# Direct tiles ahead of the products, value products in one step, full column transposes, and weight sums through GpSimd's queue: one edit to a one-layer encoder kernel

## The chip, the core and the metric

The kernel runs on one NeuronCore of a Trainium2 chip. The time is the device time of one execution in microseconds (us). Three runs of the kernel as it was gave 2321.19, 2312.80 and 2321.06 us, a median of 2321.06 us. A fourth execution was recorded by the hardware profiler, and every row of a profile below is from such a recording.

The engines are named as the profile names them: PE (TensorE's matmuls), PEld (its weight loads), DVE (VectorE), ACT (ScalarE), POOL (GpSimd) and SP (the queue of SyncE, from which most DMA transfers start). Each engine runs its instructions in its own fixed order. An instruction that has to wait holds back everything behind it on the same engine.

## What is computed

One layer of a streaming encoder is applied to a prompt of 2048 rows and to 8 short samples of 16 rows (one more tile of 128 rows), 1024 features wide:

```
z = x @ w_in                        # q, k, v, output gate, 8 gate columns, attention q, k, v
hm = mlstm_chunkwise(...)           # 4 heads x 128, carries a matrix state from chunk to chunk
ha = sliding-window attention(...)  # 8 query heads, 2 key/value heads x 64, with sinks
h = layer_norm(alpha * x + concat(hm, ha) @ w_out)
y = layer_norm(alpha * h + conv_ffn(h))   # up 1024 -> 5632, causal conv, silu gate, down 2816 -> 1024
```

All of it is float32. Large products are made from three matmuls on split operands (a high part and a remainder of each operand), so every operand of PE is first split: ACT writes the high part and DVE the remainder. The groups of large products are also made with seven block products instead of eight, in the manner of Strassen and Winograd, so sums of blocks of x and of the weights have to be made beforehand. These sums are DVE's work.

## The kernel before

**Stages.** The input products (stage I, function `i_dense`) go over 4 blocks of 512 rows (block 0 has the sample tile as well). Each block goes through 5 groups of weight columns (g = 0 to 4), and a group is seven block products with the numbers 1 to 7 (s). Beside them stand the "direct" tiles (`i_direct`, 24 matmuls of 264 columns, L730): the gate columns, the attention keys and the attention values of 128 rows. Then come the output product with the first layer norm (`o_block`), the up projection (matmuls at L1873) and the down projection (L2083).

**Chains.** While the input and output products run, two chains of small steps are woven between them: `m_chain` for the mLSTM and `a_chain` for the attention, each tile after tile (16 prompt tiles). A chain is a generator. At each `yield` it says what its step costs PE, how long its next step should wait, and how many of the 5 rotating PSUM banks it needs. `Chains.weave` keeps a planned time and takes a step when both wait and banks are due (`HOLDS` is the planned time that a bank stays in use). So the order of PE's instructions is fixed by this plan when the program is built. If an operand is late on the chip, PE stands still.

**The start.** Before the change `i_begin` puts tiles 2 and 3 of block 0 first (L343), then product (0,0,1), the sample tile, and the other products. Tiles 0 and 1 of a block come at the end of that block, together with tiles 2 and 3 of the next (L362 to L364). `i_dense` writes out the loads of the start by hand (L592 to L615): weights of the direct tiles (`next_raw`, `next_split`), the four raw quarters of x (`x_load`, buffers `xr1` to `xr4`, 512 KB each), and their splits and sums (`x_steps`). The `passages` (L618) say after which product of the last group each split or sum for the next block is made.

**Attention.** In `swa` (L1271) the scores of a tile are softmaxed; then the weights are transposed for each of the two key tiles (`ppt`, L1342), copied by ACT (`pth`, L1343), and multiplied with the values (`ppo`, L1348). The product for one key tile comes one step after its transposes, so the value products of a tile are two groups of 4 PE instructions with other work between. They use half of the array's columns (64 of 128). `scores` also copies a sink column into the score buffer on GpSimd (L1297).

**mLSTM columns.** `m_cols` (L1020) transposes a row buffer `ay` of 36 partitions into columns (`pcol`, L1024), once for each of 17 tiles. `m_rows` sends a row vector to DRAM and back, spread over all partitions, through GpSimd's queue (`zM` at L1078, `wi` at L1080), and the next tile's `m_masked` (L1109, DVE) reads `wi`.

**Weight sums.** `d_sums` (L840) prepares sums of the down projection's weights for the third stage: step 0 loads two pieces of 512 KB (`txy`), step 1 makes four subtractions on DVE (L850 to L853), step 2 stores both (`zt`). There are 11 of these: 4 in each of blocks 2 and 3, at products 6, 5 and 3 (6, 2 and 5 in group 3), and 3 in the output stage. All of them use the raw buffers `xr1` and `xr3` and SP's queue, so the load of one waits for the store of the one before it.

Of the kernel before, what the change touches and what calls it, by code (L numbers as in the profile page):

```python
# [34 lines left out]
HOLDS = {"pm": 6500, "pgr": 4000, "pnum": 5000, "ppo": 6500}  # L35
# [169 lines left out]
class Prog:  # L205
# [131 lines left out]
    def i_begin(self):  # L337
# [196 lines left out]
    def x_load(self, b, *qs):  # L534
        for q in qs:
            self.xr[b, q] = r = self.x_raw(q)
            self.nc.sync.dma_start(r, self.a["xq"][b][(q - 1) // 2, (q - 1) % 2])

    def x_steps(self, b, *steps):
# [3 lines left out]
        for s in steps:  # L543
# [14 lines left out]
            else:  # L558
# [3 lines left out]
                n = 4 if (b, s) == (0, "b12") else 1  # L562
# [24 lines left out]
    def i_dense(self):  # L587
# [5 lines left out]
        self.x_load(0, 2)  # L593
        for _ in range(3):
            self.next_raw()
        self.x_load(0, 4)
# [3 lines left out]
        self.rope_load(IBLOCKS[0][2], 2)  # L600
# [12 lines left out]
        self.x_steps(0, 2, "t3", 7, "t2", 6)  # L613
# [4 lines left out]
        passages = [{1: ["load"], 7: ["t3", 7], 6: ["t2", 6], 3: [3, "t4"], 4: ["b12", "t1"]},  # L618
                    {1: ["load"], 6: ["t3"], 7: [7, "t2"], 5: [6], 3: [3, "t4"], 4: ["b12", "t1"]}]
        sums = 0  # L620
        after = None
        for item in self.items:
# [9 lines left out]
            if item[0] == "t":  # L632
# [33 lines left out]
            if (g, s) == (1, 6):  # L666
                self.rope_load(IBLOCKS[b][0], 2)
            if g == last and b + 1 < nb:
                if s == 7:
                    self.rope_load(IBLOCKS[b + 1][2], 2)  # L670
# [11 lines left out]
            if b >= nb // 2 and g < last:  # L682
# [1503 lines left out]
```

## Time and profile before

| | us |
|---|---|
| runs | 2321.19, 2312.80, 2321.06 |
| median | 2321.06 |
| profiled execution, its own time | 2316.15 |
| its span, first to last instruction | 2314.3 |
| mean granted clock of PE | 0.996 |
| moved by DMA in the span | 632.38 MB, mean 273 GB/s |

In this execution the direct tiles ran at 5.9 to 17.2 us (tiles 2 and 3), 21.3 to 24.4 (the sample tile), 155 to 167, 290 to 302 and 455 to 467 (four tiles each) and 623 to 629 us (the last two). The output stage began at 628.8 us on PE.

How to read the rows. In a timeline a row is: start in us, duration in us, engine, line, operation, output <- inputs, shape, count of instructions merged into the row, and in brackets the idle time of the engine just before and what ended it. A matmul's duration includes its way through the array, so that matmuls overlap; what one costs is seen from the start of the next. In a table of windows each engine has its busy time in the stretch, then come the granted clock of PE (1.00 is full speed), the share of the time in which the DMA engines were busy, and GB/s. In a row of a tile or a line the three numbers are shortest, median and longest in ns.

### The profile page before, as it was taken

How to read it: one execution, taken by the hardware profiler on the slowest of the kernel's cores; microseconds unless marked ns; L12 is line 12 of the kernel's file. 1: busy time of each engine (PE TensorE's matmuls, PEld its weight loads, DVE VectorE, ACT ScalarE, POOL GpSimd, SP SyncE). 2: the span in 40 equal slices, each digit the busy share in tenths (PEclk: the TensorE clock that was granted, in tenths of full speed). 3: DMA queues.
4: the chain of work that ended last, by engine and by line, in shares of the span. 5: the costliest groups of instructions: out<-in, count | busy, mean ns of one | idle time of the engine just before them, and what ended most of it. 6: DMA issues, size and time to landing. Idle time of an engine off the chain costs nothing.

```text
span 2314.3 us, 39788 instructions
## 1 busy us (share of the span) xinstructions
PE 2281.9 (99%) x14293; PEld 2094.9 (91%) x14293; DVE 1808.1 (78%) x3075; ACT 1269.0 (55%) x2377; POOL 279.5 (12%) x509
## 2 busy tenths in 40 slices
PE   8999999999999999999999999999999999999998
PEld 8999989989877778999999999999999978888876
DVE  8777687787688888998788777678766786895987
ACT  5453466776766655555656555555555544444442
POOL 0001000000011212121002000013111200100200
PEclk9999999999999999999999999999999999999999
DMA  7888999999977757888778889978898776756743
GB/s 276 287 308 297 301 309 336 314 310 342 315 269 240 240 201 270 303 319 311 276 289 274 306 304 311 315 264 287 312 294 261 225 282 208 261 175 215 255 157 108
DMA packets 300166, 632.38 MB, mean 273 GB/s; under 512 B 47869, under 2 KB 141121, under 8 KB 299969
## 3 DMA queue, kind: packets, MB, share of 16 engines
q1 hardware_dynamic: 295296, 616.14, 77.9%
q0 software_dynamic: 3520, 10.56, 1.4%
q10 hardware_dynamic: 1152, 3.15, 0.4%
q8 instruction: 113, 1.85, 0.3%
q14 instruction: 85, 0.69, 0.1%
HBM read 458.11 MB, written 171.64 MB: 272 GB/s over the span
## 4 chain that ended last, share of the span: by engine, by line
PE 76%; DVE 5%; DMA 4%; issue 2%; ACT 1%; SPq 0%; POOL 0%; DVEq 0%; ACTq 0%; POOLq 0%
PE dps L1873 19%; PE fup L1873 19%; PE dps L704 7%; PE dps L2083 6%; PE fht L2083 6%; PE fup L2083 6%; PE dps L222 2%; PE dps L224 2%; PE dps L223 2%; PE ppo L1348 1%; PE psc L1303 1%; PE ppt L1342 1%; DVE w L218 1%; PE fht L1697 1%; DMA txy<-wdn 0%
## 5 line engine op out<-in xcount | busy, mean ns | idle before, releaser
L1873 PE MATMUL dps<-hh,uw 128*128 128x384 f32 (+1 forms) x1848 | 478.7, 328 | 2.0 <-DVE u L1904 2.0
L1873 PE MATMUL fup<-hh,uw 128*128 128x384 f32 (+1 forms) x1848 | 478.2, 328 | 1.5 <-ACT ua L1894 1.5
L1873 PEld LDWEIGHTS dps<-hh,uw 128*128 128x128 f32 x1848 | 330.5, 188 | 2.2 <-DVE u L1904 2.2
L1873 PEld LDWEIGHTS fup<-hh,uw 128*128 128x128 f32 x1848 | 330.0, 188 | 2.0 <-ACT ua L1894 1.9
L1930 DVE SCALAR_TENSOR_TENSOR cc<-u,cw,cc 128x768 f32<-128x768 f32 (+1 forms) x264 | 258.1, 978 | 64.9 <-ACT cc L1928 55.5
L1873 PE MATMUL fup<-hl,uw 128*128 128x384 f32 (+1 forms) x924 | 302.5, 327 | 1.7 <-DVE hl L218 1.7
L1873 PE MATMUL dps<-hl,uw 128*128 128x384 f32 (+1 forms) x924 | 302.8, 328 | 0.0
L704 PE MATMUL dps<-w,oh 128*128 128x256 f32 x1344 | 254.3, 284 | 0.7 <-DVE zev L777 0.7
L217 ACT CAST uw<-wraw 128x1024 fp32r<-128x1024 f32 x126 | 123.0, 979 | 223.8 <-PE dps L2083 120.1
L218 DVE TENSOR_TENSOR w<-wraw,w 128x1024 fp32r<-128x1024 f32 (+2 forms) x167 | 189.4, 1141 | 56.1 <-ACT w L217 48.9
L217 ACT CAST w<-wraw 128x1024 fp32r<-128x1024 f32 (+2 forms) x167 | 163.0, 985 | 107.3 <-PE dps L704 38.9
L704 PEld LDWEIGHTS dps<-w,oh 128*128 128x128 f32 x1344 | 210.5, 188 | 11.8 <-issue 8.1
L218 DVE TENSOR_TENSOR uw<-wraw,uw 128x1024 fp32r<-128x1024 f32 x126 | 142.4, 1131 | 65.7 <-ACT uw L217 65.5
L704 PE MATMUL dps<-w,ol 128*128 128x256 f32 x672 | 187.8, 279 | 0.0
L704 PE MATMUL dps<-oh,w 128*128 128x256 f32 x896 | 170.9, 285 | 6.6 <-ACT mr L1153 3.8
L1873 PEld LDWEIGHTS fup<-hl,uw 128*128 128x128 f32 x924 | 173.5, 188 | 2.4 <-DVE hl L218 2.3
L2083 PE MATMUL fup<-uw,fu 128*128 128x512 f32 x726 | 174.2, 396 | 0.6 <-DVE uw L218 0.6
L1873 PEld LDWEIGHTS dps<-hl,uw 128*128 128x128 f32 x924 | 173.8, 188 | 0.0
L2083 PEld LDWEIGHTS fup<-uw,fu 128*128 128x128 f32 x726 | 136.6, 188 | 34.1 <-DVE uw L218 1.1
L2083 PE MATMUL dps<-uw,fu 128*128 128x512 f32 x660 | 165.3, 396 | 1.1 <-DVE uw L218 1.1
L1928 ACT ACTIVATE cc<-u,cw 128x768 f32<-128x768 f32 (+1 forms) x132 | 132.2, 1002 | 57.8 <-DVE u L1910 28.5
L704 PEld LDWEIGHTS dps<-oh,w 128*128 128x128 f32 x896 | 142.2, 191 | 13.1 <-ACT mr L1153 4.1
(318 smaller groups left out, 4567.0 us busy)
## 6 DMA issues: line engine op xcount, KB each, us to landing
uw<-zw SPq DMA_DIRECT2D x176, 512.0 KB, 5.1
zw<-uw SPq DMA_DIRECT2D x88, 512.0 KB, 3.7
w<-zws SPq DMA_DIRECT2D x72, 512.0 KB, 6.2
wv<-wup SPq DMA_DIRECT2D x66, 512.0 KB, 5.0
wraw<-wi SPq DMA_DIRECT2D x65, 512.0 KB, 5.1
wraw<-zt SPq DMA_DIRECT2D x60, 512.0 KB, 4.3
wraw<-wdn SPq DMA_DIRECT2D x45, 512.0 KB, 4.3
wraw<-wo SPq DMA_DIRECT2D x40, 512.0 KB, 4.5
```

The costliest lines, as they stand in the source:

```text
L217: nc.scalar.copy(hi, src)
L218: nc.vector.tensor_sub(lo, src, hi.bitcast(F32))
L222: mm(out, ah, bh, start=start, stop=False)
L223: mm(out, ah, bl, start=False, stop=False)
L224: mm(out, al, bh, start=False, stop=stop)
L704: mm(o, l, r, start=s in (1, 7) and c == k == i == 0, stop=k == 3 and i == 2, skip_group_check=True)
L1303: nc.tensor.matmul(ps[kvh][:, j, :nk], q[rs, j0 + j], k[rs, sel], start=i == 0, stop=i == 2)
L1342: nc.tensor.transpose(pp[:, j * P:(j + 1) * P], scs[j // 2][:, 2 * kvh + j % 2, kt * P:(kt + 1) * P], self.ident)
L1873: mm(ps, l[:, k], r[:, k], start=s in (1, 7) and k == 0 and i == 0, stop=k == 3 and i == 2, skip_group_check=True)
L1928: S.activation(c[:, v], u[:, 2:2 + n], AF.Identity, bias=w[3], scale=w[2])
L1930: V.scalar_tensor_tensor(c[:, v], u[:, i:i + n], w[i], c[:, v], op0=ALU.mult, op1=ALU.add)
L2083: mm(ps, l[:, k, c], r[:, k], start=s in (1, 4, 7) and u == 0 and k == 0 and i == 0, stop=u == nu - 1 and k == n - 1 and i == 2, skip_grou ...
```

## The change

- **Order of the direct tiles.** All four tiles of a block come before its products. For block 0, tiles 0 and 1 lead: their first halves (x quarter 1), then their second halves (quarter 3), then tiles 2 and 3. The last two tiles at the end of stage I are gone, and with them one load of the direct weights.
- **Loads and splits follow that order.** Quarter 1 of block 0 is loaded in two parts and split in four. `passages` split quarters 1 and 2 of the next block after product 2 (5 in block 0).
- **Value products.** Both groups of a tile are issued together after both transposes; the waits, banks and `HOLDS["ppo"]` of the plan change with them.
- **Column transposes.** `ay` has 128 partitions, and the transpose is a full 128 by 128.
- **Weight sums.** Load, subtraction and store of one sum are at products 4 of the group before, 5 and 3 (1, 5, 3 in group 0; 2 and 5 in group 3). They use two buffer pairs in turn, and GpSimd's queue.
- **Sink column.** It is copied by ACT, after the maxima.

```diff
-HOLDS = {"pm": 6500, "pgr": 4000, "pnum": 5000, "ppo": 6500}
+HOLDS = {"pm": 6500, "pgr": 4000, "pnum": 5000, "ppo": 5000}
...
-                it += [("t", 0, i, -1) for i in (2, 3)]
+                it += [("t", 0, i, -1) for i in (1, 2, 3)]
...
-            it += [("t", b, i, b) for i in (0, 1)]
             if b + 1 < nb:
-                it += [("t", b + 1, i, b) for i in (2, 3)]
+                it += [("t", b + 1, i, b) for i in range(4)]
...
+            n = 2 if (b, q) == (0, 1) else 1
+            for i in range(n):
+                k = slice(i * 4 // n, (i + 1) * 4 // n)
+                self.nc.sync.dma_start(r[:, k], x[:, k])
...
         self.next_raw()
-        self.x_load(0, 2)
-        for _ in range(3):
+        self.x_load(0, 1)
+        self.next_raw()
+        self.x_load(0, 3)
+        for _ in range(2):
             self.next_raw()
-        self.x_load(0, 4)
+        self.x_load(0, 2, 4)
...
         self.next_split()
-        self.x_steps(0, "b12")
-        for _ in range(3):
+        self.x_steps(0, 1)
+        self.next_split()
+        self.x_steps(0, 2)
+        for _ in range(2):
             self.next_split()
-        self.x_steps(0, 3)
+        self.x_steps(0, "b12", 3)
         self.x_single(1, 2)
-        self.x_load(0, 1)
         self.next_raw()
-        self.x_load(0, 3)
-        self.x_steps(0, 1)
         self.advance()
-        self.x_steps(0, 2, "t3", 7, "t2", 6)
+        self.x_steps(0, "t3", 7, "t2", 6)
...
-        passages = [{1: ["load"], 7: ["t3", 7], 6: ["t2", 6], 3: [3, "t4"], 4: ["b12", "t1"]},
-                    {1: ["load"], 6: ["t3"], 7: [7, "t2"], 5: [6], 3: [3, "t4"], 4: ["b12", "t1"]}]
+        passages = [{1: ["load"], 7: ["t3", 7], 6: ["t2", 6], 2: [1], 5: [2], 3: [3, "t4"], 4: ["b12", "t1"]},
+                    {1: ["load"], 6: ["t3"], 7: [7, "t2"], 5: [6], 2: [1, 2], 3: [3, "t4"], 4: ["b12", "t1"]}]
...
+                if b == 0 and ti == 1:
+                    for h in range(2):
+                        for i in range(2):
+                            yield from self.i_direct(b, i, e, self.ib[i * 2], (h,))
+                    self.i_keys(b, 0, self.ib[0])
+                    self.i_keys(b, 1, self.ib[2])
+                    self.advance()
+                    continue
...
-                if ti == 1:
-                    if b + 1 < nb:
-                        self.x_steps(b + 1, 1, 2)
-                    else:
-                        self.release(4)
-                    after = [6, b + 1]
-                elif ti == 3 and b or ti == 4:
+                if ti == 3 and b or ti == 4:
...
-            if (g, s) == (1, 6):
-                self.rope_load(IBLOCKS[b][0], 2)
+            if (g, s) == (last, 4):
+                after = [8, b + 1]
...
-                        self.x_load(b + 1, 1, 2, 3, 4)
+                        self.x_load(b + 1, 1, 3, 2, 4)
...
-            if b >= nb // 2 and g < last:
-                steps = (6, 2, 5) if g == last - 1 else (6, 5, 3)
-                if s in steps:
-                    self.d_sums(sums, steps.index(s))
-                    sums += s == steps[2]
+            if b >= nb // 2:
+                if (g, s) == (0, 1) or s == 4 and g < last - 1:
+                    self.d_sums(sums, 0)
+                    sums += 1
+                elif g < last and s in ((2, 5) if g == last - 1 else (5, 3)):
+                    self.d_sums(sums - 1, 2 if s == 3 or g == last - 1 and s == 5 else 1)
...
-            self.txy = x, y = [self.xp.tile([P, D], F32, name="txy", tag=f"xr{q}", bufs=1) for q in (1, 3)]
-            nc.sync.dma_start(x, self.a["wdn"][k])
-            nc.sync.dma_start(y, self.a["wdn"][NK2 + k])
+            self.txy = x, y = [self.xp.tile([P, D], F32, name="txy", tag=f"xr{q}", bufs=1) for q in ((1, 3), (2, 4))[k % 2]]
+            nc.gpsimd.dma_start(x, self.a["wdn"][k])
+            nc.gpsimd.dma_start(y, self.a["wdn"][NK2 + k])
...
-        nc.sync.dma_start(self.zt[0, k], x)
-        nc.sync.dma_start(self.zt[1, k], y)
+        nc.gpsimd.dma_start(self.zt[0, k], x)
+        nc.gpsimd.dma_start(self.zt[1, k], y)
...
-        self.ay = [self.one(f"ay{i}", [36, P]) for i in range(2)]
+        self.ay = [self.one(f"ay{i}", [P, P]) for i in range(2)]
...
-        ps = self.bank([P, 36], "pcol")
-        nc.tensor.transpose(ps, self.ay[i], self.ident[:36, :36])
+        ps = self.bank([P, P], "pcol")
+        nc.tensor.transpose(ps, self.ay[i], self.ident)
...
-            nc.gpsimd.tensor_copy(sc[:, :, N:N + 1].rearrange("p (k j) o -> p k (j o)", k=2), sink)
...
+            nc.scalar.copy(sc[:, :, N:N + 1].rearrange("p (k j) o -> p k (j o)", k=2), sink)
...
-            if kt:
-                po = po or self.bank([P, 512], "ppo")
-                for kvh in range(2):
-                    w = self.kv[slots[kt - 1]][:, P + 64 * kvh:P + 64 * kvh + 64]
-                    nc.tensor.matmul(po[64 * kvh:64 * kvh + 64], w, pts[:, kvh], start=kt == 1, stop=kt == nk)
-            pts = new
+            pts.append(new)
...
-            yield (860 if kt < nk else 0) + (1400 if kt else 0), 0 if kt == nk else 1500 if kt else 3000, 2 * (kt + 1 < nk) + (kt == 0)
+            yield 860, 3000 if kt + 1 == nk else 1500, 1 if kt + 1 == nk else 2
+        po = self.bank([P, 512], "ppo")
+        for kt in range(nk):
+            for kvh in range(2):
+                w = self.kv[slots[kt]][:, P + 64 * kvh:P + 64 * kvh + 64]
+                nc.tensor.matmul(po[64 * kvh:64 * kvh + 64], w, pts[kt][:, kvh], start=kt == 0, stop=kt + 1 == nk)
+        yield 1400 * nk, 0
```

More of the change, by code (lines that the diff above doesn't have):

```diff
@@ L599, in i_dense @@
         self.angles = {}
-        self.rope_load(IBLOCKS[0][2], 2)
+        for i in (0, 2):
+            self.rope_load(IBLOCKS[0][i], 2)
         self.rope_load(NPT, 1)
         self.next_split()
-        self.x_steps(0, "b12")
-        for _ in range(3):
+        self.x_steps(0, 1)
+        self.next_split()
+        self.x_steps(0, 2)
+        for _ in range(2):
             self.next_split()
-        self.x_steps(0, 3)
+        self.x_steps(0, "b12", 3)
         self.x_single(1, 2)
-        self.x_load(0, 1)
         self.next_raw()
-        self.x_load(0, 3)
-        self.x_steps(0, 1)
         self.advance()
-        self.x_steps(0, 2, "t3", 7, "t2", 6)
+        self.x_steps(0, "t3", 7, "t2", 6)
         self.x_single(4)
@@ L665, in i_dense @@
                 self.t_setup()
-            if (g, s) == (1, 6):
-                self.rope_load(IBLOCKS[b][0], 2)
+            if (g, s) == (last, 4):
+                after = [8, b + 1]
             if g == last and b + 1 < nb:
                 if s == 7:
-                    self.rope_load(IBLOCKS[b + 1][2], 2)
+                    for i in (0, 2):
+                        self.rope_load(IBLOCKS[b + 1][i], 2)
                 for x in passages[b > 0].get(s, ()):
@@ L716, in i_product, with i_direct @@
                     yield 645
-    def i_direct(self, b, ti, e, ps):
+    def i_direct(self, b, ti, e, ps, halves=(0, 1)):
         mm = self.nc.tensor.matmul
-        for k in range(KD):
+        for k in [4 * h + i for h in halves for i in range(4)]:
             wh, wl = [w[:, k % 2] for w in self.wu["g", e, k // 2]]
@@ L1334, in swa @@
         yield 0, 4200, 2 + 2 * (self.a_load is not None)
-        po = pts = None
-        for kt in range(nk + 1):
-            new = self.work("pth", [P, 2, 512], bufs=2) if kt < nk else None
-            for kvh in range(2) if kt < nk else ():
+        pts = []
+        for kt in range(nk):
+            new = self.work("pth", [P, 2, 512], bufs=2)
+            for kvh in range(2):
                 pp = self.bank([P, 512], "ppt")
@@ L1353, in swa @@
                 self.chains.t += 550
-            yield (860 if kt < nk else 0) + (1400 if kt else 0), 0 if kt == nk else 1500 if kt else 3000, 2 * (kt + 1 < nk) + (kt == 0)
+            yield 860, 3000 if kt + 1 == nk else 1500, 1 if kt + 1 == nk else 2
+        po = self.bank([P, 512], "ppo")
+        for kt in range(nk):
+            for kvh in range(2):
+                w = self.kv[slots[kt]][:, P + 64 * kvh:P + 64 * kvh + 64]
+                nc.tensor.matmul(po[64 * kvh:64 * kvh + 64], w, pts[kt][:, kvh], start=kt == 0, stop=kt + 1 == nk)
+        yield 1400 * nk, 0
         nc.scalar.copy(mix.rearrange("p a b -> p (a b)"), po)
```

8 lines of the change are left out of this document (4 added, 4 removed).

## The prediction

> **What bounds the kernel now.** I read the page's busy shares first, then a table of windows, then the waits and the timeline around each stretch in which PE stood still. The profiled execution took 2316.15 us by its own time, 1.85 us more than its span, and I make the sum against 2316.15; the median of the runs shown, 2321.06, lies 4.9 above it.
>
> ```profile
> PE 2281.9 (99%) x14293; PEld 2094.9 (91%) x14293; DVE 1808.1 (78%) x3075; ACT 1269.0 (55%) x2377; POOL 279.5 (12%) x509
> ```
>
> The reader is to see that PE is the bound nearly everywhere. The edit removes no large matmul, so it can win only what PE loses: idle time (32 us in the span), a lower clock, and gaps between starts that "busy" hides. The windows of the start show the first two:
>
> ```profile
> 0.00:20.00 20.00, 15.53 (x82) 13.53 (x83) 14.79 (x36) 11.55 (x23) 0.31 (x5) 0.91 0.88 331
> 20.00:40.00 20.00, 17.50 (x139) 16.54 (x138) 20.00 (x25) 11.55 (x15) 0.00 (x0) 0.99 0.64 222
> 40.00:60.00 20.00, 19.31 (x150) 18.86 (x150) 13.66 (x15) 8.74 (x13) 0.00 (x0) 0.92 0.78 268
> ```
>
> PE is idle for 4.47, 2.50 and 0.69 us. Of the first, 1.98 come before the warm-up and stay, so 5.7 us are open. From 20 to 40 us DVE is busy for 20.00 of 20: there VectorE is the bound, making splits and sums. Finer windows show the clock:
>
> ```profile
> 8.90:12.20 3.30, 1.69 (x12) 1.27 (x11) 2.77 (x4) 2.19 (x3) 0.00 (x0) 1.00 1.03 403
> 12.20:15.60 3.40, 3.40 (x18) 3.40 (x17) 3.03 (x8) 2.58 (x7) 0.00 (x0) 0.53 1.02 418
> 36.10:39.50 3.40, 1.80 (x14) 1.41 (x13) 3.40 (x6) 2.58 (x3) 0.00 (x0) 1.00 0.98 390
> 39.50:43.00 3.50, 3.50 (x18) 3.50 (x19) 3.34 (x5) 1.31 (x2) 0.00 (x0) 0.53 0.72 256
> 326.30:329.70 3.40, 0.16 (x2) 0.00 (x0) 3.33 (x14) 1.07 (x3) 0.00 (x0) 1.00 0.78 217
> 329.70:333.10 3.40, 2.80 (x13) 2.80 (x14) 3.31 (x9) 2.26 (x7) 0.00 (x0) 0.52 1.10 340
> ```
>
> Each time PE was busy for only about half of some 3.4 us, or less, the next stretch of that length was granted 0.52 or 0.53 of the clock. That costs about 3.4 x 0.47 = 1.6 us each time.
>
> **The start: 5.5 us won.** The change puts two more direct tiles ahead of the products. One costs 2.9 us of PE, as the sample tile shows, whose successor starts at 24.21:
>
> ```profile
> 21.32 3.05 PE L730 MATMUL pg<-w,xs 128*128 128x264 f32 x24
> ```
>
> So PE gets 5.8 us of work that it had at the end of stage I. DVE gets two rotations of keys with it, 1.0 us each by the first and the last of four instructions:
>
> ```profile
> 13.42 0.23 DVE L868 TENSOR_TENSOR rb<-zev,ropet 128x64 f32<-128x64 f32 x1 [0.26 <-ACT zev L738]
> ...
> 14.14 0.29 DVE L871 TENSOR_TENSOR zev<-zev,rb 128x128 f32<-128x128 f32 x1
> ```
>
> DVE therefore gains 5.8 - 2.0 = 3.8 us on PE. That covers the 2.50 + 0.69 us of the second and third window with 0.6 to spare, and with the wait in 36.1 to 39.5 goes the low clock behind it (1.6). Of the 2.5 us in the first window I count the spare 0.6 alone, since the weights still have to be split, and its low clock as staying. Sum 3.2 + 1.6 + 0.6 = 5.4, rounded to 5.5. Best end: all of 5.7 + 2 x 1.6 = 8.9. Worst end: VectorE stays the bound, which gives 3.8, and the two x quarters that now stand ahead of the product weights in SP's queue (1 MB at the 403 GB/s above, 2.6 us) delay the first product: 1.2.
>
> The Trainium skill, page "TensorE: Matmul & The Clock Gate", section "Why this matters for your kernels", asks for no idle gap of PE over about 3 us if the clock is to stay up. By that rule the first window, whose 1.6 us of idle time lie in pieces between 12 matmuls, would not have lost the clock, and short new waits there would not either: 1.6 us more won, 2300 us. The rows above speak against it.
>
> **The weight sums: 6.5 us won.** At 321 to 325 us DVE stands before a sum whose load has not landed:
>
> ```profile
> 325.20 0.69 DVE L850 TENSOR_TENSOR txy<-txy 128x512 f32<-128x512 f32 x1 [3.92 <-DMA txy<-wdn]
> ...
> 328.63 0.17 ACT L1153 ACTIVATE mr<-pnum 128x2 f32<-128x2 f32 x1 [3.17 <-DVE bst L1150]
> 328.71 1.04 ACT L217 CAST w<-wraw 128x1024 fp32r<-128x1024 f32 x1
> ...
> 330.30 0.58 PE L704 MATMUL dps<-oh,w 128*128 128x256 f32 x1 [3.85 <-ACT mr L1153]
> ```
>
> Read it downward: behind DVE's sum wait the statistics of a head; ACT waits for these, with a weight split queued behind; PE waits for that split. This one wait costs 3.85 and the low clock 1.6 (the last window above). The same wait comes twice more, and PE's waits in 300 to 900 us hold what may follow from them:
>
> ```profile
> 516.33 0.69 DVE L851 TENSOR_TENSOR txy<-txy 128x512 f32<-128x512 f32 x1 [4.37 <-DMA txy<-wdn]
> ...
> 539.60 0.69 DVE L850 TENSOR_TENSOR txy<-txy 128x512 f32<-128x512 f32 x1 [4.22 <-DMA zqk<-zev]
> ```
>
> ```profile
> PE pht L1176 <- DVE ql L218: 1.0, 1, 1.0
> PE ppo L1348 <- ACT pth L1343: 0.6, 1, 0.6
> ```
>
> Together 3.85 + 1.6 + 1.0 + 0.6 = 7.05. Today a load waits in SP's queue for the store of the sum before it, then has two or three products of time. With two buffer pairs nothing holds it, and it is issued three or four products ahead: at least 3 x 24 matmuls x 0.12 us = 8.6 us, against landings of
>
> ```profile
> DMA to landing us min/median/max: 3.3/5.2/9.8
> ```
>
> I take 6.5, since the longest landing is over 8.6. Ends: 0 (another wait takes each place) and 7.05.
>
> **Shapes on the array: 5.0 us won.**
>
> ```profile
> 403.05 1.04 PE L1342 MATMUL ppt<-ident,sc 128*128 128x128 f32 x8
> 404.02 1.08 PE L1348 MATMUL ppo<-pth,kva 128*64 128x512 f32 x4
> 405.03 0.38 PE L704 MATMUL dps<-w,oh 128*128 128x256 f32 x1
> ...
> 407.57 0.28 PE L704 MATMUL dps<-w,oh 128*128 128x256 f32 x1
> 407.78 0.25 PE L1024 MATMUL pcol<-ident,ay 36*128 36x36 f32 x1
> 407.96 1.08 PE L1348 MATMUL ppo<-pth,kva 128*64 128x512 f32 x4
> ```
>
> ```profile
> 404.50 0.60 PE L1348 MATMUL ppo<-pth,kva 128*64 128x512 f32 x2
> ```
>
> Full transposes start 0.11 apart (8 take 0.97, with 0.20 for the last). A change of shape, to 64 columns or to 36 rows, makes the next start come after 0.20 or 0.21, and PE counts as busy all the while. A group of value products takes 1.01 (404.02 to 405.03), its two pairs 0.48 apart. Four pairs in one go take 3 x 0.48 + 0.53 = 1.97 against 2.02 for two groups, and one entry falls away, worth 0.08 (0.20 against the usual 0.12) to 0.20; I take 0.15, near the middle. For the 15 tiles with two key tiles: 15 x 0.20 = 3.0. The column transpose costs 0.21 + 0.18 - 0.20 (the value product's own entry) = 0.19 where a value product follows, and 0.11 as a full transpose: 0.08 won, or 0.16 where ordinary products follow (0.39 against 0.23). For 17 of them 1.4 to 2.7, and I take 2.0. Ends: 0.75, if only 15 x 0.05 is real and the gaps have another cause, and 15 x 0.25 + 2.7 = 6.5.
>
> **What it adds: 2.5 us lost.** The 44 transfers of the sums leave SP's queue for POOL's. Each holds POOL for 0.58 us, by rows of the same size:
>
> ```profile
> L2126 POOL DMA_DIRECT2D y<-yacc x12: 531/576/606, 1992.7 to 2191.5; - x12
> ```
>
> POOL is busy 12%, so its time is no matter, but its order is: a store of a sum waits on POOL for DVE, and behind it stand the m chain's row transfers and the power (L1160) on which ACT's scaling waits. One new wait of the size of 1.5 us is my charge. At the end of stage I the two last tiles covered 5.8 us of loads and splits for the output stage; I charge 1.0, from 0 to 2.9, half the cover, because one load and four splits of direct weights go too. The sink copies on ACT, the moved rotation tables, one later pair of x splits and the new planned holds I cost at nothing: ACT is busy 55%, and these stand products ahead of their use. Ends for this part: 0 and 6.
>
> **Sum.** 2316.15 - 5.5 - 6.5 - 5.0 + 2.5 = 2301.65, so 2302 us: 0.6% under the profiled execution and 0.8% under the median. All best ends give 2293.7, all worst ends 2320.
>
> **Rivals.** *VectorE stays the bound.* The start gives 1.2, DVE finds another wait in each place of the sums (0), the shapes give 5.0, 2.5 is lost: 2312.5. For it speaks DVE's 20.00 of 20; against it that in 300 us and later DVE waits for this load and not for work.
>
> *The shapes are not the cause of the gaps* (the change doesn't do what it says): 0.75 in place of 5.0, so 2306. The regular 0.20 at each such start speaks against it.
>
> *GpSimd's queue makes the m chain late: slower than before.* Its rows are these:
>
> ```profile
> L1080 POOL DMA_DIRECT2D wi<-zM x16: 563/569/604, 287.6 to 807.8; - x16
> ...
> DMA to landing us min/median/max: 3.6/5.0/7.6
> ```
>
> ```profile
> 646.27 0.69 DVE L1109 TENSOR_TENSOR dt<-k_mcau,wi 128x512 f32<-128x512 f32 x1 [2.14 <-DMA wi<-zM]
> ```
>
> DVE has already waited for this transfer once, so there is little room. Put the four issues of a sum (2.3 us) and a landing of 512 KB ahead of it, and DVE stops as at 325 us, at 3.85 + 1.6 = 5.45 each time. From the third such wait on (16.4) the 14.5 won are gone; five of the eight sums in blocks 2 and 3 give 2302 + 27 = 2329. Against it speaks that a load is now issued half a group before it is needed, and may stand behind `wi` as well as ahead.
>
> The Trainium skill, page "SBUF — State Buffer", section "SBUF: two separate sides", says that DMAs from GpSimd's queue get their descriptors from GpSimd and starve while VectorE holds a shared port in some of its modes. That is this rival's mechanism; the 0.58 us above, beside a busy VectorE, show no starving.
>
> **Chances and range.** The forecast, 2302: 0.54. VectorE stays the bound, 2312.5: 0.24. The shapes: 0.10. GpSimd's queue: 0.12. A measurement of this kernel can tell about 0.5% (11.6 us) from no change, so against the median the line is at 2309.5. Faster: the forecast and 0.06 of the shapes' rival, 0.60; within: 0.28; slower: 0.12. The range runs from 2293, all best ends, to 2317, which takes in the first two rivals with some 4 us of scatter and leaves out GpSimd's queue and the tails.
>
> **What would show it.** Right: no wait of PE over 0.5 us between 20 and 45 us and full clock there; no DVE wait for `txy` in 300 to 600 us, and none of 3.85 on PE; one group of 8 value products for a tile, about 1.97 us from its start to the next; column transposes 0.11 apart from what follows. Wrong: DVE full and PE waiting for splits until 45 us; waits for `wi` at L1109, or for POOL's power before L1166, above the 2.14 of today; a wait of PE where the output stage begins.

## The result: 0.7% slower

In six executions of each kernel on one chip, the changed kernel takes 2333.12 us (median, 2329.06 to 2338.66), the kernel before 2319.01 us (2312.80 to 2321.19). The ratio is 1.0069, with a 95% interval of 1.0049 to 1.0090: slower, by 14 us at the medians. The prediction was 2302, faster. The profiled execution took 2333.21 us (span 2331.4), against 2316.15 before: 17.06 more.

Where do they lie? The start is the place to look first, since there the prediction saw its surest gain. Here are the busy shares of the page, and the same three windows as before:

```profile
PE 2283.5 (98%) x14293; PEld 2100.6 (90%) x14293; DVE 1812.9 (78%) x3071; ACT 1269.8 (54%) x2405; POOL 288.0 (12%) x521
```

```profile
0.00:20.00 20.00, 16.18 (x102) 14.63 (x103) 13.70 (x33) 12.27 (x26) 0.31 (x5) 1.00 0.87 332
20.00:40.00 20.00, 18.63 (x157) 18.43 (x156) 19.97 (x31) 9.52 (x15) 0.00 (x0) 1.00 0.58 186
40.00:60.00 20.00, 17.10 (x142) 16.50 (x141) 18.27 (x37) 9.53 (x15) 0.00 (x0) 1.00 0.91 319
...
148.50:152.40 3.90, 1.40 (x12) 1.20 (x11) 2.29 (x3) 1.65 (x3) 0.31 (x1) 1.00 0.64 231
152.40:155.80 3.40, 3.40 (x20) 3.40 (x19) 1.57 (x3) 0.63 (x1) 0.00 (x0) 0.58 0.76 233
...
326.60:330.40 3.80, 1.17 (x11) 0.97 (x9) 3.80 (x7) 1.28 (x4) 1.90 (x4) 1.00 0.80 168
330.40:337.20 6.80, 5.25 (x24) 5.28 (x25) 4.40 (x14) 2.43 (x8) 1.22 (x3) 0.50 1.00 357
```

The start's clock is full now (0.91, 0.99 and 0.92 before): its two slow stretches are gone, although DVE is still busy for 19.97 of 20 us. But the chain stage has new ones. At 149 and at 327 us PE stood still for most of some 4 us, and the next 3.4 and 6.8 us were granted 0.58 and 0.50 of the clock.

The first output product and GpSimd's closing DRAIN mark the rest. These are two rows of the changed kernel's table by source line, and the DRAIN of the kernel before (L2182 is there the same line):

```profile
L222 PE MATMUL dps<-w,oh x272: 387/394/776, 640.1 to 920.3; 128*128 128x512 f32 x136
...
L2192 POOLq DRAIN  x3: 40/93/8222, 2322.4 to 2331.2; - x3
```

```profile
L2182 POOLq DRAIN  x3: 45/93/4627, 2308.8 to 2314.0; - x3
```

The output stage begins at 640.1 us instead of 628.8: stage I lost 11.3. The DRAIN, which begins at GpSimd's last instruction, starts 13.6 us later, and it takes 8.22 us instead of 4.63, 3.6 more. 13.6 + 3.6 = 17.2 is the whole difference. So the loss is made in the chain stage, and a fifth of it at the very end. The low clock has a part in it: between the warm-up and the last matmul the granted clock stood at 0.50 for 27.3 us in the changed kernel and for 13.7 us before, which is worth 6.8 us.

The loads of the weight sums did not become free. DVE waits for them in 300 to 600 us seven times (table of waits: us in total, times, longest), 14.7 us in all; before the change it was 15.2 us, in seven times too:

```profile
DVE txy L859 <- DMA txy<-wdn: 9.1, 5, 2.6
DVE txy L860 <- DMA txy<-wdn: 5.6, 2, 4.3
```

One of these, followed through the timeline of the changed kernel (DVE's rows, then PE's):

```profile
325.76 0.69 DVE L859 TENSOR_TENSOR txy<-txy 128x512 f32<-128x512 f32 x1 [2.35 <-DMA txy<-wdn]
...
327.50 0.69 DVE L861 TENSOR_TENSOR txy<-txy 128x512 f32<-128x512 f32 x1
...
328.22 0.69 DVE L862 TENSOR_TENSOR txy<-txy 128x512 f32<-128x512 f32 x1
...
331.17 0.68 DVE L1141 TENSOR_TENSOR dt<-pscore,dt 128x512 f32<-128x512 f32 x1
...
331.95 2.06 PE L1220 MATMUL pnum<-v,dt 128*128 128x129 f32 x8 [4.18 <-issue]
```

Read it downward. DVE stops 2.35 us for a load and then works off the sum's subtractions (L859, L861, L862) between the pieces of both chains. The masked scores (L1141), which PE needs, come only at 331.17, and PE has stood for 4.18 us. That is the picture of 325 us in the kernel before, with another chain piece at its end. (The table puts PE's wait down to "issue"; that it ends with the masked scores is read from the two rows.)

### The profile page after: what moved, and what is told of

Read it like the earlier page. It is cut to its first block, busy times and chain, and to the rows that moved or that the text cites. A ratio compares the mean times of both kernels' runs of the same rounds, so it can differ in the third digit from the quotient of the medians.

```text
span 2331.4 us, 39736 instructions
## 1 busy us (share of the span) xinstructions
PE 2283.5 (98%) x14293; PEld 2100.6 (90%) x14293; DVE 1812.9 (78%) x3071; ACT 1269.8 (54%) x2405; POOL 288.0 (12%) x521
## 5 line engine op out<-in xcount | busy, mean ns | idle before, releaser
L2093 PEld LDWEIGHTS dps<-uw,fu 128*128 128x128 f32 x660 | 123.9, 188 | 31.5 <-DVE uw L218 1.5
```

The costliest lines, as they stand in the source:

```text
L2093: mm(ps, l[:, k, c], r[:, k], start=s in (1, 4, 7) and u == 0 and k == 0 and i == 0, stop=u == nu - 1 and k == n - 1 and i == 2, skip_grou ...
```

## The experiments

Ratios are to the kernel before on the same chip, with 95% intervals. 0.001 is 2.3 us.

**First question: which part loses?** Four kernels, each with one part undone or one part alone.

e1 leaves everything changed, but SP issues the sums' transfers:

```diff
-            nc.gpsimd.dma_start(x, self.a["wdn"][k])
+            nc.sync.dma_start(x, self.a["wdn"][k])
...
-        nc.gpsimd.dma_start(self.zt[0, k], x)
+        nc.sync.dma_start(self.zt[0, k], x)
```

> The changed kernel, with the 44 transfers of the weight sums issued by SP again; buffer pairs and places of the three steps stay as changed. Theory Q (GpSimd's queue costs the time): the closing DRAIN of GpSimd falls from 8.22 us back to about 4.6, so 3.5 us come back at the end, and with the order on POOL free some of the 11.3 us that stage I lost come back: 2322 to 2329. Theory O (the new order at the passages and the plan around it cost the time): only the end changes or nothing does, 2329 to 2333; DVE waits for txy stay at 15 to 20 us in sum.

Measured: 2316.73 us, 1.0004 (0.9993 to 1.0016). All of the loss is back, more than theory Q asked for. PE's instructions stand in the same order in both kernels, so neither the plan nor the shapes are the cause of the loss in the changed kernel: the sums' transfers on GpSimd's queue are, with what goes with them. DVE's order is not the same: with SP's queue the sums' subtractions stand later, behind pieces of the chains that they precede in the changed kernel.

With PE's order the same, each matmul can be compared from trace to trace. At 331 us of e1 the changed kernel lags 6.8 us behind it, but at 412 us 0.1, because e1 has a stall of its own in between. So the wait followed above is not what is left at the end. From 489 to 538 us the lag goes from 0.3 to 8.0, and it is 7.2 to 8.9 from there to 773 us. These are DVE's and PE's rows of the changed kernel in that stretch, and the two windows behind them:

```profile
507.45 0.69 DVE L860 TENSOR_TENSOR txy<-txy 128x512 f32<-128x512 f32 x1 [4.30 <-DMA txy<-wdn]
...
518.79 0.77 PE L1220 MATMUL pnum<-v,dt 128*128 128x129 f32 x2 [2.79 <-DVE asm L1327]
```

```profile
514.50:518.10 3.60, 1.50 (x14) 1.30 (x12) 3.60 (x11) 2.84 (x9) 0.55 (x1) 1.00 0.66 199
518.10:524.90 6.80, 6.11 (x28) 6.14 (x29) 5.91 (x15) 6.05 (x16) 1.17 (x3) 0.50 0.97 356
```

DVE stops 4.30 us for a load. PE waits 1.01, 1.05 and 2.79 us for results of DVE that come after it, and loses 6.80 x 0.50 = 3.4 us by the clock, 8.3 us together.

e2 undoes the sums wholly (L849 to L865 and their calls as before):

```diff
-            if b >= nb // 2:
-                if (g, s) == (0, 1) or s == 4 and g < last - 1:
+            if b >= nb // 2 and g < last:
+                steps = (6, 2, 5) if g == last - 1 else (6, 5, 3)
```

> The changed kernel, with the weight sums wholly as before (one buffer pair, three steps per group, SP's queue); direct tiles, shapes and the sinks' copies stay as changed. Theory Q: the start's 4.8 us and the shapes' 5 us are left as a gain, less the wait of 2.5 us and its low clock 1.7 at the first passage: about 2314. Theory O: the new stalls between 140 and 860 us are still there and only the tail's 3.5 us come back: about 2329.

Measured: 2317.97 us, 1.0013 (1.0000 to 1.0026). Theory O falls. But theory Q's 2314 isn't there either: start and shapes together win nothing.

e3 is the kernel before with the shapes alone, e4 with the order of the direct tiles alone:

```diff
-        ps = self.bank([P, 36], "pcol")
+        ps = self.bank([P, P], "pcol")
...
+        yield 1400 * nk, 0
```

> The kernel before, with only the shapes changed: the value products of a tile in one step with the hold that goes with it, and column transposes of 128 rows. Theory S (the shapes are worth what the gaps say): 5 us faster, 2314, with the row of 8 value products at 1.9 us from its start to the next. Rival (one long step moves the chain's pieces so that PE meets later results): the same gaps vanish, but waits of PE for ACT and DVE and low clock take them back: 2319 or more.

```diff
-                it += [("t", 0, i, -1) for i in (2, 3)]
+                it += [("t", 0, i, -1) for i in (1, 2, 3)]
```

> The kernel before, with only the order of the direct tiles changed (start, passages, x loads, rotation tables). Theory O: the start wins 4.8 us, the first passage loses 2.5 by the late direct weights and 1.7 by the clock, and more stalls at later passages: 2322 to 2328. Theory Q: the start's gain less the first passage's loss is all there is: about 2318.

Measured: e3 2321.49 us, 1.0018 (1.0006 to 1.0030), slower, as its rival had it; e4 2318.35 us, 1.0007 (0.9995 to 1.0019), as theory Q had it. So two parts on which I had counted 10.5 us give nothing or less by themselves. Both come back below.

**Second question: what of GpSimd's queue?** e8 is the sums' part alone on the kernel before. e5 keeps only the loads on GpSimd, e6 only the stores. e7 keeps all transfers there, but holds the subtractions behind the weight split that was issued last:

```diff
-        nc.gpsimd.dma_start(self.zt[0, k], x)
+        nc.sync.dma_start(self.zt[0, k], x)
```

> The changed kernel, with only the 22 loads of the weight sums on GpSimd's queue; their 22 stores are issued by SP. Its subtractions stand in DVE's stream as in the changed kernel: early, ahead of the m chain's and the attention's pieces. Theory V (a load on GpSimd's queue puts the sums earlier into DVE's order, and DVE then stands before a load that has not landed with the chains queued behind): nearly as slow as the changed kernel, 2326 to 2331, the closing DRAIN about half way, 6.4 us. Theory P (the order on POOL, stores ahead of the m chain's transfers and power): about 2318.

```diff
-            nc.gpsimd.dma_start(x, self.a["wdn"][k])
+            nc.sync.dma_start(x, self.a["wdn"][k])
```

> The changed kernel, with only the 22 stores of the weight sums on GpSimd's queue; their loads are issued by SP. Its subtractions stand in DVE's stream about as in the kernel with all sums on SP. Theory V: 2317, and 1.8 more where the closing DRAIN grows to 6.4 us: 2317 to 2320. Theory P: stores that wait for DVE still stand ahead of the m chain's transfers on POOL: 2325 to 2330.

```diff
-        nc.vector.tensor_sub(lo, src, hi.bitcast(F32))
+        self.lv = nc.vector.tensor_sub(lo, src, hi.bitcast(F32))
...
+            with self.tc.issue_after(self.lv.ins):
+                V.tensor_sub(x[:, l], x[:, r], x[:, l])
```

> The changed kernel, all 44 transfers on GpSimd's queue, but the four subtractions of a sum may stand in DVE's stream only behind the weight split that was issued last before them. Theory V: with the sums out of the chains' way DVE's waits for txy fall below 10 us (19 in the changed kernel), and all but the DRAIN's 3.6 us comes back: 2320 to 2323. Theory P or slower transfers: 2330 to 2335 as before.

```diff
+            self.txy = x, y = [self.xp.tile([P, D], F32, name="txy", tag=f"xr{q}", bufs=1) for q in ((1, 3), (2, 4))[k % 2]]
+            nc.gpsimd.dma_start(x, self.a["wdn"][k])
```

> The kernel before, with only the weight sums changed: two buffer pairs, earlier loads, GpSimd's queue. Theory V and theory P alike: the loss is this part's alone, so about 2317 + 14 = 2331, with the DRAIN at 8.2 us. Rival (the sums only hurt together with the new order of the direct tiles, whose x splits stand in the same buffers): 2320 to 2324.

Measured: e5 2333.20 us, 1.0074 (1.0052 to 1.0096); e6 2324.50, 1.0034 (1.0019 to 1.0050); e7 2331.93, 1.0064 (1.0040 to 1.0087); e8 2332.23, 1.0069 (1.0046 to 1.0092). The part alone costs what the whole change costs. PE's order in e8 is that of the kernel before, and the low clock lasts 13.7 us in both, so neither the plan nor the clock by itself is the cause. The loads alone do it, against theory P. The stores alone cost half: 2324.50 lies above theory V's range, and its interval reaches into theory P's 2325 to 2330 (their road was not followed further). And e7 goes against theory V: in 270 to 900 us DVE waits for no sum's load any more, and the time stays.

The trace of e5 shows the worst case of the early sums, in the stretch in which the changed kernel falls behind too. POOL's rows come first, then DVE's, then PE's:

```profile
502.94 0.59 POOL L854 DMA_DIRECT2D txy<-wdn  x1 [7.07 <-DMA zt<-txy]
504.20 0.54 POOL L853 DMA_DIRECT2D txy<-wdn  x1 [0.68 <-DMA zt<-txy]
505.43 0.53 POOL L854 DMA_DIRECT2D txy<-wdn  x1 [0.69 <-DMA zt<-txy]
...
511.68 0.69 DVE L860 TENSOR_TENSOR txy<-txy 128x512 f32<-128x512 f32 x1 [8.50 <-DMA txy<-wdn]
...
513.93 0.27 DVE L1085 TENSOR_TENSOR ay<-pgr,r_b 4x128 f32<-4x128 f32 x1
...
514.26 2.07 PE L1137 MATMUL pscore<-qk 128*128 128x128 f32 x8 [5.02 <-DVE ay L1085]
```

One load stands on POOL for 7.07 us until a store from the same buffer pair has landed, and the two behind it in the queue start that much later. So two pairs are not enough: the load of sum k waits for the store of sum k-2. DVE, whose order puts the sum early, stops for 8.50 us with the m chain's row behind it, and PE stands for 5.02.

In e7 DVE no longer stops there. There are waits on POOL instead (timeline, POOL's rows first, then who waits for them):

```profile
365.82 0.53 POOL L853 DMA_DIRECT2D txy<-wdn  x1 [3.46 <-DMA zt<-txy]
368.94 0.54 POOL L854 DMA_DIRECT2D txy<-wdn  x1 [2.58 <-DMA zt<-txy]
369.49 1.05 POOL L1170 TENSOR_TENSOR ms<-mr,mhalf 128x4 f32<-128x4 f32 x1
...
370.57 0.40 ACT L1176 ACTIVATE hn<-hn,ms 128x128 f32<-128x128 f32 x1 [4.06 <-POOL ms L1170]
...
541.40 0.53 POOL L853 DMA_DIRECT2D txy<-wdn  x1 [4.00 <-DMA zt<-txy]
541.92 0.53 POOL L1088 DMA_DIRECT2D zM<-r_M  x1
...
556.71 0.69 DVE L1119 TENSOR_TENSOR dt<-k_mcau,wi 128x512 f32<-128x512 f32 x1 [5.73 <-DMA wi<-zM]
```

Loads that wait for a store hold POOL for 3.46 and 2.58 us. Behind them stands the m chain's power (L1170), and ACT waits 4.06 for it. At 541 us the same wait stands ahead of the m chain's row transfer, and DVE waits 5.73 for its second half. This last wait is the one of the prediction's third rival.

To tell the two roads apart: e17 takes only the row transfers off POOL, e13 does that with the subtractions held.

```diff
-        self.nc.gpsimd.dma_start(self.zM[i][0], self.M)
+        self.nc.sync.dma_start(self.zM[i][0], self.M)
```

> The changed kernel with the subtractions of the sums held behind a weight split, and the m chain's row transfers zM and wi issued by SP; GpSimd keeps the sums' 44 transfers and the power. Theory P1 (the row transfers behind the sums on POOL are the rest of the loss): the 5.73 us wait of DVE for wi goes, and 2320 to 2324 are left with the DRAIN. Theory P2 (it is the power, which still stands on POOL behind loads that wait for a store): little changes, 2328 to 2332, with ACT still waiting for POOL's ms before hn.

> The changed kernel, all sums on GpSimd's queue and their subtractions where they stand in it, with only the m chain's row transfers zM and wi issued by SP. If the row transfers behind the sums are the loss: as with the held subtractions, 2320 to 2323. If DVE's early sums alone cost as much: 2328 to 2333, with DVE's waits for txy at 15 us or more. Between them if the two share it.

Measured: e13 2321.66 us, 1.0019 (1.0009 to 1.0029); e17 2335.17, 1.0079 (1.0066 to 1.0092). Holding the sums alone wins nothing (e7), freeing the row transfers alone wins nothing (e17), both together win back 10 to 14 us. So either road is enough to keep the loss: in e17 DVE waits 28.2 us for the sums' loads (270 to 900 us; 19.0 in the changed kernel), in e7 not at all.

Theory P2 falls with e13: ACT still waits 28.4 us in 15 pieces for the power there, against 31.1 in 16 in the kernel before, and it costs little. From 360 to 420 us PE is busy for 54.57 of 60 us in e13 and for 54.62 in e7, so the wait for the power shown above is not what e7 loses by. Matmul by matmul, e7 falls behind e13 mainly at 424 to 460 us (from 4.5 to 8.7 us) and at 549 to 585 (8.2 to 14.9), the second time behind the wait for `wi`; at the output stage the lag is 8.7. What starts the first of the two was not followed, so the second road is shown in part only.

At most 1 us of e13's rest is its DRAIN, and 2.6 of what it wins over e7. These are the DRAIN rows of e6 and of e13:

```profile
L2192 POOLq DRAIN  x3: 40/93/6424, 2317.6 to 2324.9; - x3
```

```profile
L2193 POOLq DRAIN  x3: 40/93/5607, 2313.0 to 2319.1; - x3
```

Against the 4.63 of the kernel before, e13 has 12 more transfers on GpSimd's queue (44 of the sums less 16 `zM` and 16 `wi`), e6 has 22 more and the changed kernel 44. That is 0.98, 1.80 and 3.60 us more, each time 0.082 us a transfer. (e17, with 12 more as well, has the 5.607 of e13.)

**Third question: why do the shapes win nothing?** e9 is the column transposes alone, e10 the one step alone, e14 the one step with more planned time before a tile's transposes:

```diff
-        nc.tensor.transpose(ps, self.ay[i], self.ident[:36, :36])
+        nc.tensor.transpose(ps, self.ay[i], self.ident)
```

> The kernel before, with only the 17 column transposes widened to 128 rows. The order of PE's pieces stays, apart from a few neighbours. Theory S (a gap closed is time won): 2.0 us faster, between 1.4 and 2.7, so 2314 to 2315. Theory C (in the chain stage a small gain of PE is taken back where a chain's result comes late): 2317, no change.

```diff
-            pts = new
+            pts.append(new)
...
+        yield 1400 * nk, 0
```

> The kernel before, with only the value products of a tile in one step (with its hold of 5000). Theory S: 3 us faster, 2314. Theory C: the planned order of the pieces on PE changes, attention's exponentials meet the m chain's scaling on ACT, and a wait of PE at the transposes as long as the 3.9 us seen with both shapes comes with a low clock: 2319 to 2322.

```diff
-        yield 0, 4200, 2 + 2 * (self.a_load is not None)
+        yield 0, 6200, 2 + 2 * (self.a_load is not None)
```

> The kernel before with the value products in one step, and 6200 in place of 4200 planned before the first transposes of a tile. If the loss of 10 us is PE meeting the divided weights too early (3.6 us at 816 us, and the low clock behind it): that wait goes, 2317 to 2320. If it is the moved order as such, with other meetings in other places: 2322 to 2328.

Measured: e9 2316.24 us, 0.9996 (0.9983 to 1.0009), no difference that can be told; e10 2326.44, 1.0046 (1.0030 to 1.0063); e14 2350.19, 1.0143 (1.0123 to 1.0163). In e10's trace, as in e3's, PE meets the divided weights too early. First the row of its waits in 780 to 940 us, then its windows there:

```profile
PE ppt L1342 <- ACT sc L1320: 3.6, 1, 3.6
```

```profile
815.50:818.90 3.40, 0.72 (x5) 0.35 (x3) 3.40 (x7) 1.72 (x5) 1.02 (x1) 1.00 0.93 317
818.90:825.70 6.80, 5.83 (x21) 4.84 (x22) 5.09 (x8) 3.92 (x9) 0.00 (x0) 0.50 0.80 258
```

That is 3.6 us and 6.80 x 0.5 = 3.4 us of clock, which the kernel before doesn't lose there. But e14, meant to mend this, fell wide of both expectations: 33 us. Part of it lies where the output stage waits for its last rows, as its window 900 to 920 us shows:

```profile
900.00:920.00 20.00, 10.29 (x36) 7.16 (x36) 5.95 (x9) 6.17 (x9) 0.00 (x0) 0.83 0.84 301
```

PE works 10.29 of 20 us, where it worked 18.89 before, and the clock was 0.83: some 12 of the 33 us. That the moved tiles are the cause of the rest is not shown; of the two plans tried, neither helped. e10's profiled execution took 2319.86 us, the least of its seven; the trace therefore explains only part of e10's loss. The rest stays open.

**Fourth question: do the harmless parts add?** e11 is the sums' part alone with SP's queue, e12 adds the sinks' copies on ACT and the column transposes:

```diff
+            self.txy = x, y = [self.xp.tile([P, D], F32, name="txy", tag=f"xr{q}", bufs=1) for q in ((1, 3), (2, 4))[k % 2]]
             nc.sync.dma_start(x, self.a["wdn"][k])
```

> The kernel before, with the weight sums' two buffer pairs and earlier steps, all their transfers issued by SP. If the queue is the cause of the loss, the 15.6 us of the same part on GpSimd's queue go whole, and what the prediction wanted of the pairs is left to be seen: the wait of 3.9 us before the second sum with its low clock goes, 2311 to 2315. If the early loads are the cause: 2325 or more.

```diff
-            nc.gpsimd.tensor_copy(sc[:, :, N:N + 1].rearrange("p (k j) o -> p k (j o)", k=2), sink)
+            nc.scalar.copy(sc[:, :, N:N + 1].rearrange("p (k j) o -> p k (j o)", k=2), sink)
```

> The kernel before, with the parts that lost nothing by themselves as far as seen: pairs with SP's queue, the sinks' copies on ACT, column transposes of 128 rows; direct tiles and value products as before. If the gains add: 2317 - 3 - 2 = 2312 or less. If the chain stage takes them back: 2316 to 2319.

e15 is e1 without the one step, e16 is e15 with the sums as before:

```diff
-            pts.append(new)
+            pts = new
...
-        yield 1400 * nk, 0
```

> The changed kernel with the sums' transfers issued by SP and the value products stepped as before. By itself the one step cost 10.7 us, the pairs on SP's queue 4.2, the direct tiles 1.7, the column transposes nothing. If the losses add: e1's 2317.6 less 10.7, 2307 to 2310. If they are meetings of the chains that each order makes anew: 2315 to 2322.

```diff
-            self.txy = x, y = [self.xp.tile([P, D], F32, name="txy", tag=f"xr{q}", bufs=1) for q in ((1, 3), (2, 4))[k % 2]]
+            self.txy = x, y = [self.xp.tile([P, D], F32, name="txy", tag=f"xr{q}", bufs=1) for q in (1, 3)]
```

> The kernel before with the direct tiles' order, the sinks' copies on ACT and the column transposes changed; sums and value products as before. If the start's 4 us outlast the first passage once nothing else moves the chains: 2311 to 2314. If not: 2317 to 2321.

Measured: e11 2320.01 us, 1.0018 (1.0004 to 1.0031); e12 2316.84, 1.0003 (0.9992 to 1.0013); e15 2317.40, 1.0002 (0.9991 to 1.0012); e16 2316.67, 1.0002 (0.9989 to 1.0014). They don't add. e11 shows that the pairs win nothing even on SP's queue; it missed both of its expectations. The one step, which cost 10.7 us by itself, costs nothing between e15 (without) and e1 (with).

One loss is common to all the kernels so far that have the new direct order: the passage from block 0 to block 1. From 140 to 160 us PE works 17.4 to 18.3 of 20 us in them, and 20.00 in the kernel before and in e8. e18 is e15 with one more edit. The first direct weight of that passage is loaded into a buffer of the m chain that is not in use yet:

```diff
+        own = u[0] == "g" and u[1] == 0 and u[2] == 0
...
-            self.raw_of[u] = e = self.raw_slot([P, 2, 264])
+            self.raw_of[u] = e = [self.tp.tile([P, 4, HT], F32, name="wraw", tag="qk", bufs=2).rearrange("p a b -> p (a b)")[:, :528].rearrange("p (a b) -> p a b", a=2), False] if own else self.raw_slot([P, 2, 264])
```

> The changed kernel with the sums on SP's queue and value products stepped as before, and the first direct weight of the first passage loaded into a buffer that is free there, so that the four loads are issued some 2 to 4 us earlier. If the start's gain is lost to these late weights: the 2.3 us wait of PE for the copy and the low clock behind it go, 2313. If another wait takes their place: 2316 to 2318.

Measured: 2310.71 us, 0.9977 (0.9966 to 0.9988). It is the only version whose interval lies below the kernel before: 5 us less than that, and 21 less than the change by the two ratios. PE's order is that of e15. The same stretch in e15, with SP's loads, ACT's split and PE's wait:

```profile
140.27 0.45 SPq L457 DMA_DIRECT2D wraw<-wg  x1
145.61 0.92 SPq L457 DMA_DIRECT2D wraw<-wg  x2
...
149.88 0.63 ACT L217 CAST w<-wraw 128x528 fp32r<-128x528 f32 x1 [3.46 <-DMA wraw<-wg]
150.42 0.58 ACT L780 COPY zev<-dps 128x512 f32<-128x512 f32 x1
151.05 0.39 PE L713 MATMUL dps<-w,oh 128*128 128x256 f32 x1 [2.27 <-ACT zev L780]
```

```profile
140.00:160.00 20.00, 17.73 (x137) 17.53 (x136) 13.09 (x15) 11.54 (x16) 0.62 (x2) 0.91 0.81 272
```

And in e18, its loads and the same window:

```profile
136.31 0.33 SPq L458 DMA_DIRECT2D wraw<-wg  x1
140.97 1.20 SPq L458 DMA_DIRECT2D wraw<-wg  x1
```

```profile
140.00:160.00 20.00, 20.00 (x171) 20.00 (x170) 15.22 (x17) 12.37 (x19) 0.62 (x2) 1.00 0.89 303
```

In e15 ACT stands 3.46 us before a direct weight that has not landed, with a copy queued behind it that frees PE's bank; PE waits 2.27 and loses clock. With the loads some 4 us earlier PE works 20.00 of 20 at full clock. The medians lie 6.7 us apart, the two profiled executions only 1.8 (e15's, 2312.58, is the least of its eleven), so the traces show this one wait and not the whole difference.

## Why the prediction was wrong

**Start, 5.5 us: a gain of that size came, by another road, and the passage took it.** The direct tiles of block 1 started at 155.0 us before. They begin as follows in the changed kernel and in e18, both of which have 5.8 us more direct work done by then:

```profile
L739 PE MATMUL dps<-w,oh x64: 280/284/287, 160.5 to 171.9; 128*128 128x264 f32 x64
```

```profile
L740 PE MATMUL dps<-w,oh x64: 280/284/287, 155.8 to 167.2; 128*128 128x264 f32 x64
```

e18 keeps 155.0 + 5.8 - 155.8 = 5.0 us, near the 5.5; the changed kernel keeps 0.3. That e18 comes so near is in part luck. The prediction had 3.8 us from PE's idle time and 1.6 from one low clock; by the windows of the first 155 us PE is idle for 7.0 us in e18 and was for 8.4 before, 1.4 us less, and the other 3.6 are the clock that was missing in the first three windows before (20 x 0.09, 20 x 0.01 and 20 x 0.08). In the changed kernel PE is idle in the first 60 us for 8.09, where it was for 7.66: DVE stays full until 40 us, and PE waits 1.37 us for it at 33.5 and 0.79 at 41.7. That was the sign named for the first rival, that VectorE stays the bound.

The step that failed in the time is "one later pair of x splits ... I cost at nothing: these stand products ahead of their use". What does not stand ahead is the direct weights, whose loads come some 4 us later than before (136.5 us, now 140.8) and stop ACT.

**Weight sums, 6.5 us: the step that failed most.** "With two buffer pairs nothing holds it" is wrong in the traces: in the changed kernel loads stood on POOL three times, 5.71 us the longest, for the store of the sum before the last (7.07 in e5, 3.46 in e7). Alone (e8) the part costs 1.0069, some 16 us, where the prediction had 6.5 won and 2.5 lost; on SP's queue it costs 1.0018 (e11). The reason given for the gain was partly wrong too: I took the wait of 3.85 at 325 us as removable, while DVE's order of both chains and the sums puts another in its place.

**Shapes, 5.0 us: right on PE, without effect on the time.** Two places of the changed kernel's timeline:

```profile
385.88 0.27 PE L1033 MATMUL pcol<-ident,ay 128*128 128x128 f32 x1
385.91 0.36 PE L713 MATMUL dps<-w,oh 128*128 128x256 f32 x1
...
386.79 1.94 PE L1363 MATMUL ppo<-pth,kva 128*64 128x512 f32 x8
388.66 0.39 PE L713 MATMUL dps<-w,oh 128*128 128x256 f32 x1
```

The eight value products take 1.87 us to the next start (1.97 predicted), the column transpose 0.03 (0.11). The gaps are closed: PE's busy time rose by only 1.6 us (2281.9, now 2283.5) although the clock cost it 6.8, so that some 5 us of it are gone, by estimate. Yet e10 and e3 are slower. (e9 hardly tests its part: a value product still follows 13 of its 17 transposes and then starts 0.20 later, and its interval still holds the 2.0 us.) What failed is the silent step from a gap closed on PE to time won: in e3 and e10 PE meets a chain's result too early and waits 3.9 and 3.6 us for it, with a low clock behind.

**What it adds, 2.5 us: too small by far.** One new wait on POOL was charged. The runs show two roads, DVE's early sums and the row transfers behind waiting loads, each enough by itself to keep the loss, the low clock behind many of the waits, and the 3.6 us by which the DRAIN grew, which I had not counted at all. The rival "GpSimd's queue makes the m chain late", 2329 us at 0.12, named the queue and came near the time, but not by the wait that it describes: in 270 to 900 us of the changed kernel DVE never waits for `wi`, and ACT waits 23.7 us for the power, less than before. DVE stops for the sums' own loads. The wait for `wi` shows only when the sums are held (e7), where a load stands ahead of it and waits for a store. So the nearness of 2329 is in part luck.

On starving, the row of the sums' transfers in the changed kernel, then in e1, answers:

```profile
DMA to landing us min/median/max: 2.9/6.0/7.8
```

```profile
DMA to landing us min/median/max: 3.0/6.4/10.1
```

Through GpSimd's queue the transfers land no later than through SP's. The Trainium skill, page "DMA: Bandwidth & Descriptors", section "Issuing engines are not separate DMA queues", says that all issuing engines share the same DMA engines and that a second issuer saves only issue time. These rows agree, and it speaks against the move: there was little to win by it.

## What to carry to other kernels

Before a transfer moves to another engine's queue, list what stands behind it on that engine, and for each transfer what it waits for; an idle engine is no free queue if its few instructions lie on a chain. Buffer pairs give freedom only if the store of the pair lands before its next load is due. And a gap closed on the bounding engine is won only where the next operand is already there: look at the first wait after it, and mend that (e18) before counting the gain.

## What the runs showed of the hardware

The closing DRAIN of GpSimd grows by 0.082 us for each transfer on its queue. Before the change it ended together with SP's own (2313.4 us); in the changed kernel SP's came at 2327.5 and GpSimd's ended at 2330.7, so the growth lengthened the program, by some 3.2 us. The transfers differ in size (512 KB for a sum's, 258 KB for `wi`), and the growth goes by their number.

The clock falls without any long gap. In the changed kernel PE waits only 0.39, 0.44 and 0.48 us here, between four transposes:

```profile
347.50:350.90 3.40, 2.08 (x13) 1.37 (x12) 0.64 (x2) 3.28 (x8) 1.18 (x3) 1.00 1.03 402
350.90:354.30 3.40, 3.40 (x16) 2.87 (x17) 2.78 (x5) 3.40 (x10) 0.00 (x0) 0.50 1.05 416
```

PE is busy for 2.08 of 3.40 us, and the next 3.40 run at 0.50. The Trainium skill, page "TensorE: Matmul & The Clock Gate", section "Why this matters for your kernels", asks only for no gap of over about 3 us; the rows speak against that. The same page of the Trainium skill, section "Part 4: PE-mode transpose", says that transposes do not count as PE busy in the same way. That would fit this window, and no run here tells it from the waits: in the same trace PE was busy for only 1.87 of 3.40 us from 507.9 to 511.3, with four transposes too, and the next 3.40 us had the full clock.
